# Splitting weights into high and low parts by casting and adding DMAs instead of on VectorE, in a two-block transformer kernel

## The chip, the core and the metric

The kernel runs on one core of a Trainium2 chip. A core has TensorE (PE in the profile, its weight loads PEld), VectorE (DVE), ScalarE (ACT), GpSimd (POOL) and SyncE (SP), each with its own in-order instruction queue; they wait for each other by semaphores only. 16 DMA engines move data between the memory off the core (DRAM in the code) and the two memories on it, SBUF and PSUM (128 partitions each; TensorE writes to PSUM). The metric is the device time of one execution in microseconds. It is given as the median of several executions; differences of about 0.2% can be told from no difference in this kernel.

## The reference

One sequence of 512 tokens with 1024 features passes two transformer blocks in float32. Cut to what matters:

```python
# block 1
h = rmsnorm(x, norm_mix)
x = x + hybrid_mixer(h, w_in, ...)            # gated spatial mixing + gated delta rule (4 heads), then @ w_out
m = rmsnorm(mem, norm_mem)                    # 256 memory tokens
x = x + memory_cross_attention(rmsnorm(x, norm_xa), m, xa_wq, xa_wk, xa_wv, xa_wo)
x = x + squared_relu_mlp(rmsnorm(x, norm_ffn), ffn_w1, ffn_w2)      # 1024 -> 4096 -> 1024
x = rmsnorm(x, norm_final)
# block 2
proj = rmsnorm(x, norm_mix_g_2) @ w_in_2      # split into the inputs of mLSTM and attention, and g_a, g_b
y_a, y_b = mlstm(...), sliding_window_attention(...)
x = x + (sigmoid(g_a) * (y_a @ w_branch_a_2) + sigmoid(g_b) * (y_b @ w_branch_b_2)) @ w_out_2
x = x + squared_relu_mlp(rmsnorm(x, norm_mlp_g_2), w_up_2, w_down_2)
x = x + sigmoid(rmsnorm(x, norm_ple_g_2) @ w_ple_gate_2) * (p_2 @ w_ple_proj_2)
out = rmsnorm(x, final_norm_g_2)
```

About 36 million float32 weights, some 146 MB, are read once each.

## The kernel before

The residual stays in SBUF as `x_fm`, 128 partitions x 8 feature tiles x 512 tokens. Every product with a weight goes through TensorE in the type `float32r`, which keeps fewer mantissa bits than float32. So both operands are held in two parts: a high part, rounded to `float32r`, and a low part, the remainder. `mm3` makes three products of them (L220 high x high, L221 and L222 the mixed ones) into one PSUM tile.

Weights are packed in DRAM in *granules* of 256 output columns x 1024 rows; `wgran` loads one in two halves of 512 KB (128 partitions x 4 k tiles x 256 columns, 4 KB per partition), each by one call of `wload`. A half goes through three tiles of the pool `wp`: the raw weight `wr` (2 buffers), the high part `wh` and the low part `wl` (3 buffers each). SP issues the load of `wr` (L200), ACT casts it to `wh` (L203), VectorE subtracts (`wl = wr - wh`, L204). There are 281 such casts and subtractions. In the first granule of all, `pieces` splits the first half into 1 and 3 k tiles, with the loads of `x` between them.

`proj_fm` multiplies a granule with the feature-major operand: two output tiles of 128 features x 512 tokens, each the sum of 8 k tiles x 3 products, so 48 products of 512 columns a granule; the second half of the granule is read last in each tile. There the weight is the stationary operand and the low part stands in L222. `proj_tm` makes token-major tiles (weight as moving operand, 256 columns; low part in L221). PSUM tiles of these projections are `psd`, three buffers. ACT and VectorE evacuate them; in the MLP (`ffn`) by a ReLU on VectorE (L804), a square on ACT (L805) and a split of the result into two parts (`split_sb`, L261 on ACT, L262 on VectorE).

POOL has little to do: sums of squares for the norms (`sq_acc`, L276), masks of the delta rule's heads (`dn_head`: `slg`, `dT`, `dA`, and the product with the gate `do`) and of the mLSTM's heads (`ml_head`: `E`, L1047), and a few others.

The order of instructions on each engine is set ahead of time by a scheduler of the framework, from dependencies, buffers and its own cost estimates. On an engine nothing passes an instruction that waits.

Of the kernel before, what the change touches and what calls it, by code (L numbers as in the profile page):

```python
# [9 lines left out]
F32 = mybir.dt.float32  # L10
F32R = mybir.dt.float32r
I32 = mybir.dt.int32
AF = mybir.ActivationFunctionType
ALU = mybir.AluOpType
AX = mybir.AxisListType
PSUM = bass.MemoryType.PSUM

P = 128
# [7 lines left out]
# columns of the packed per-feature vectors  # L26
# [8 lines left out]
# packed rows, replicated over the partitions by the load  # L35
# [8 lines left out]
# masks over [128, 128], and per-block masks over [128, 32] (one block of 32 columns per block of 32 rows)  # L44
# [20 lines left out]
class Kern:  # L65
    def __init__(self, tc, ctx, D, out, dbg=None):
# [3 lines left out]
        self.wp = ctx.enter_context(tc.tile_pool(name="wp", bufs=3))  # L70
# [27 lines left out]
    def psums(self):  # L98
        """four banks for the small products of a phase."""
        return self.tc.tile_pool(name=self.uid("pc"), bufs=2, space=PSUM)  # L100
# [4 lines left out]
    def pair(self, sl, dt=F32R):  # L105
        """[128, 8, 512] operand in two slots."""
# [51 lines left out]
    def rsqrt(self, pool, v, n, tag):  # L158
        """1/sqrt(v) of a small tile [128, n]."""
# [12 lines left out]
    def softplus(self, pool, z, n, tag):  # L172
        """max(z, 0) + log1p(exp(-|z|)) of a small tile, log1p(e) = 2 atanh(e / (2 + e))."""
# [19 lines left out]
    def wload(self, src, kt, n, pieces=None):  # L193
        """src: DRAM [128, kt, n]; kt*n <= 1056."""
        nc = self.nc
        raw = self.t(self.wp, [P, kt, n], "wr", bufs=2)
        hi = self.t(self.wp, [P, kt, n], "wh", F32R)
        lo = self.t(self.wp, [P, kt, n], "wl", F32R)
        for c, then in pieces or [(slice(0, kt), None)]:
            nc.sync.dma_start(raw[:, c], src[:, c])  # L200
            if then:
                then()
            nc.scalar.copy(hi[:, c], raw[:, c])  # L203
            nc.vector.tensor_tensor(out=lo[:, c], in0=raw[:, c], in1=hi[:, c].bitcast(F32), op=ALU.subtract)  # L204
        return hi, lo

    def wgran(self, name, g, n=256, nk=8, pieces=None):
        """granule g of a packed weight: (hi, lo) accessors over k."""
# [8 lines left out]
    def mm3(self, ps, ah, al, bh, bl, first, last):  # L217
        """ps (+)= a^T b with operands in two parts."""
# [15 lines left out]
    def proj_fm2(self, w, xh, xl, tiles, evac):  # L234
        """as proj_fm, k outermost."""
# [21 lines left out]
    def split_sb(self, hi, lo, src, scale=None):  # L257
        """hi/lo of src * scale (src in SBUF or PSUM, scale per partition)."""
# [19 lines left out]
    def tok_rs(self, acc, tag, ntt=NB, eps=EPS, mul=None):  # L278
        """acc: [128, tokens] partial sums over partitions -> rsqrt(mean + eps) per token, [128, ntt];
        mul: per-token factor [128, ntt] on the mean."""  # L280
# [8 lines left out]
    def tok_bc(self, rs, tag, ntt=NB, out=None):  # L289
        """[128 tok, ntt] -> [128, tokens] replicated over partitions."""  # L290
# [1086 lines left out]
```

## Time and profile before

| | before |
|---|---|
| three runs, median (lowest to highest) | 1759.84 us (1758.4 to 1761.03) |
| span of the profiled execution, first to last instruction | 1755.6 us |
| TensorE busy | 1718.3 us, 98% |
| VectorE busy | 1012.1 us, 58% |
| ACT busy | 720.4 us, 41% |
| POOL busy | 147.7 us, 8% |
| mean granted TensorE clock | 0.994 of full speed |
| DMA | 155.09 MB, 27.3% of 16 engines' span on SP's queue |

The profile is one execution, and its own time is the span; the runs of the median are other executions and include what lies before the first and after the last instruction. Busy times of TensorE are those of pipelined matmuls with modelled ends, so that 98% doesn't mean peak speed. In rows of groups, `out<-in` names the tiles, then come partitions x elements and the count, the summed busy time, the mean duration in ns, and the idle time of the engine just before these instructions with what ended it. In rows of waits, "A <- B: t, n, m" says that A waited for B, t us in all, n times, m at most. In rows of the timeline come the start, the duration, engine, line, operation and tiles, and in brackets the idle time before it.

### The profile page before, as it was taken

Reading aid. Unit: us, or ns where it says so; the run is one execution under the profiler, and the core shown is the slowest. Engines: PE = TensorE matmul, PEld = TensorE weight load, DVE = VectorE, ACT = ScalarE, POOL = GpSimd, SP = SyncE. Lnnn points to the kernel's source line nnn. Section 1 sums busy time; section 2 is a strip of 40 time slices with the busy share of each in tenths; the row PEclk is TensorE's granted clock in tenths of the full one; section 3 lists DMA queues with packets and bytes.
Section 4 is the critical chain, followed back from the end, with each engine's and each line's share of the span. In section 5 each row is a group of like instructions: output and inputs, shape, how many; then the busy total and the mean of one; then the engine's idle time right before and its main releaser. Section 6 shows DMA issues by size and latency. Waiting matters only on the chain.

```text
span 1755.6 us, 22644 instructions
## 1 busy us (share of the span) xinstructions
PE 1718.3 (98%) x8740; PEld 1427.2 (81%) x8740; DVE 1012.1 (58%) x2039; ACT 720.4 (41%) x1254; POOL 147.7 (8%) x126
## 2 busy tenths in 40 slices
PE   8999999999999999999999999999999999999997
PEld 6987788878888888888889877788888888888876
DVE  6898887655543434447755589735555434344446
ACT  5344544544342323234454468623234423232343
POOL 2211311201000000011000000000120000000102
PEclk9999999999999999999999999999999999999998
DMA  5222223312222332232222211233232222223231
GB/s 196 86 73 63 73 90 101 102 49 79 90 97 96 96 96 97 96 96 73 75 73 82 74 59 37 85 96 97 91 100 85 93 90 95 96 96 108 90 102 61
DMA packets 49436, 155.09 MB, mean 88 GB/s; under 512 B 9392, under 2 KB 11696, under 8 KB 49328
## 3 DMA queue, kind: packets, MB, share of 16 engines
q1 hardware_dynamic: 49328, 153.64, 27.3%
q8 instruction: 69, 1.13, 0.3%
q14 instruction: 39, 0.32, 0.1%
HBM read 151.26 MB, written 2.10 MB: 87 GB/s over the span
## 4 chain that ended last, share of the span: by engine, by line
PE 84%; DVE 10%; ACT 3%; issue 1%; POOL 0%; DMA 0%; SPq 0%; DVEq 0%; ACTq 0%; POOLq 0%
PE psd L221 25%; PE psd L222 25%; PE psd L220 25%; DVE wl L204 1%; ACT wh L203 1%; PE c L563 1%; ACT lg L1154 1%; PE m L1064 1%; PE c L512 1%; DVE S L368 1%; DVE e L319 1%; PE po L1170 0%; DVE qs L1122 0%; PE lg L1143 0%; DVE S L1176 0%
## 5 line engine op out<-in xcount | busy, mean ns | idle before, releaser
L220 PE MATMUL psd<-S,wh 128*128 128x512 f32 (+1 forms) x1968 | 770.4, 392 | 6.1 <-ACT wh L203 6.1
L222 PE MATMUL psd<-S,wl 128*128 128x512 f32 (+1 forms) x1968 | 774.0, 393 | 1.4 <-DVE wl L204 1.4
L221 PE MATMUL psd<-S,wh 128*128 128x512 f32 (+1 forms) x1904 | 747.9, 393 | 0.3 <-DVE S L265 0.3
L204 DVE TENSOR_TENSOR wl<-wr,wh 128x1024 fp32r<-128x1024 f32 (+3 forms) x281 | 349.1, 1242 | 219.7 <-ACT wh L203 218.0
L203 ACT CAST wh<-wr 128x1024 fp32r<-128x1024 f32 (+3 forms) x281 | 292.0, 1040 | 434.0 <-PE psd L221 408.1
L220 PEld LDWEIGHTS psd<-S,wh 128*128 128x128 f32 x1968 | 373.5, 190 | 86.7 <-ACT wh L203 7.0
L222 PEld LDWEIGHTS psd<-S,wl 128*128 128x128 f32 x1968 | 372.3, 189 | 80.9 <-DVE wl L204 3.2
L221 PEld LDWEIGHTS psd<-S,wh 128*128 128x128 f32 x1904 | 359.6, 189 | 78.8 <-DVE S L265 1.7
L276 POOL TENSOR_TENSOR acc<-acc,sq 128x512 f32<-128x512 f32 (+1 forms) x47 | 67.8, 1442 | 917.7 <-ACT sq L274 917.3
L401 DVE TENSOR_TENSOR x_fm<-psd,x_fm 128x512 f32<-128x512 f32 x88 | 60.7, 690 | 138.0 <-PE psd L222 137.9
L221 PE MATMUL psd<-wl,S 128*128 128x256 f32 (+2 forms) x480 | 137.7, 287 | 0.6 <-DVE wl L204 0.6
L222 PE MATMUL psd<-wh,S 128*128 128x256 f32 (+2 forms) x480 | 136.4, 284 | 0.0
L220 PE MATMUL psd<-wh,S 128*128 128x256 f32 (+2 forms) x480 | 136.3, 284 | 0.0
L804 DVE SCALAR_TENSOR_TENSOR e<-psd,bc 128x512 f32<-128x512 f32 x64 | 44.2, 691 | 112.2 <-PE psd L222 109.3
L805 ACT ACTIVATE e<-e 128x512 f32<-128x512 f32 x64 | 40.4, 632 | 135.1 <-DVE e L804 135.1
L221 PEld LDWEIGHTS psd<-wl,S 128*128 128x128 f32 x480 | 90.3, 188 | 1.6 <-DVE wl L204 1.0
L220 PEld LDWEIGHTS psd<-wh,S 128*128 128x128 f32 x480 | 90.5, 189 | 0.5
L222 PEld LDWEIGHTS psd<-wh,S 128*128 128x128 f32 x480 | 90.6, 189 | 0.3
L262 DVE TENSOR_TENSOR S<-e,S 128x512 fp32r<-128x512 f32 (+1 forms) x84 | 56.7, 675 | 49.2 <-ACT S L261 49.2
L261 ACT CAST S<-e 128x512 fp32r<-128x512 f32 (+1 forms) x84 | 50.5, 601 | 42.9 <-POOL e L929 27.1
L264 ACT ACTIVATE S<-x_fm,vec 128x512 fp32r<-128x512 f32 x40 | 28.8, 721 | 55.8 <-DVE x_fm L401 37.1
L319 DVE SCALAR_TENSOR_TENSOR e<-e,vec,e 128x511 f32<-128x511 f32 (+2 forms) x60 | 46.6, 779 | 2.6 <-ACT e L316 2.2
(411 smaller groups left out, 1456.7 us busy)
## 6 DMA issues: line engine op xcount, KB each, us to landing
wr<-in_ffn_w_dram SPq DMA_DIRECT2D x64, 512.0 KB
wr<-in_w_up_dram SPq DMA_DIRECT2D x32, 512.0 KB
wr<-in_w_down_dram SPq DMA_DIRECT2D x32, 512.0 KB
wr<-in_w_in_qk_dram SPq DMA_DIRECT2D x16, 512.0 KB
wr<-in_w_in_v_dram SPq DMA_DIRECT2D x12, 512.0 KB
wr<-in_xa_wk_dram SPq DMA_DIRECT2D x8, 512.0 KB
wr<-in_xa_wv_dram SPq DMA_DIRECT2D x8, 512.0 KB
wr<-in_xa_wq_dram SPq DMA_DIRECT2D x8, 512.0 KB
```

Source lines behind the costliest of these rows:

```text
L203: nc.scalar.copy(hi[:, c], raw[:, c])
L204: nc.vector.tensor_tensor(out=lo[:, c], in0=raw[:, c], in1=hi[:, c].bitcast(F32), op=ALU.subtract)
L220: mm(ps, ah, bh, start=first, stop=False)
L221: mm(ps, ah, bl, start=False, stop=False)
L222: mm(ps, al, bh, start=False, stop=last)
L261: nc.scalar.copy(hi, src)
L262: nc.vector.tensor_tensor(out=lo, in0=src, in1=hi.bitcast(F32), op=ALU.subtract)
L276: eng.tensor_tensor(out=acc, in0=acc, in1=sq, op=ALU.add)
L319: nc.vector.scalar_tensor_tensor(out=c[:, s:], in0=xr[:, :T - s], scalar=w(j), in1=c[:, s:], op0=ALU.mult, op1=ALU.add)
L401: self.nc.vector.tensor_tensor(out=self.x[:, o], in0=ps, in1=self.x[:, o], op=ALU.add)
L804: nc.vector.scalar_tensor_tensor(out=t, in0=ps, scalar=0.0, in1=bc, op0=ALU.max, op1=ALU.mult)
L805: nc.scalar.activation(t, t, AF.Square)
```

## The change

`wload` no longer has a raw tile in the pool, except where `pieces` is given (the first half granule, whose raw tile lies in the slot S8). In all other calls a DMA issued by POOL loads the weight straight into `wh`, with the cast to `float32r` on the way; ACT writes the negated high part into `wl`; and a second DMA issued by POOL reads the same raw weight from DRAM again and adds it onto `wl`. The pool `wp` has 4 buffers of each tile instead of 3. The rest of the difference is comments taken out, by which line numbers move.

```diff
-        self.wp = ctx.enter_context(tc.tile_pool(name="wp", bufs=3))
+        self.wp = ctx.enter_context(tc.tile_pool(name="wp", bufs=4))
...
     def wload(self, src, kt, n, pieces=None):
         nc = self.nc
-        raw = self.t(self.wp, [P, kt, n], "wr", bufs=2)
         hi = self.t(self.wp, [P, kt, n], "wh", F32R)
         lo = self.t(self.wp, [P, kt, n], "wl", F32R)
-        for c, then in pieces or [(slice(0, kt), None)]:
-            nc.sync.dma_start(raw[:, c], src[:, c])
-            if then:
-                then()
-            nc.scalar.copy(hi[:, c], raw[:, c])
-            nc.vector.tensor_tensor(out=lo[:, c], in0=raw[:, c], in1=hi[:, c].bitcast(F32), op=ALU.subtract)
+        if pieces:
+            raw = self.slot(8, [P, kt, n])
+            for c, then in pieces:
+                nc.sync.dma_start(raw[:, c], src[:, c])
+                if then:
+                    then()
+                nc.scalar.copy(hi[:, c], raw[:, c])
+                nc.vector.tensor_tensor(out=lo[:, c], in0=raw[:, c], in1=hi[:, c].bitcast(F32), op=ALU.subtract)
+            return hi, lo
+        nc.gpsimd.dma_start(hi, src)
+        nc.scalar.activation(lo, hi.bitcast(F32), AF.Copy, scale=-1.0)
+        nc.gpsimd.dma_start(lo, src, accum_op=ALU.add)
         return hi, lo
```

In the built program 279 of 281 half granules take the new way: 279 casts and 279 subtractions go, 279 scaled copies on ACT and 558 DMAs on POOL come, and SP loses 279 loads. The products on TensorE are the same in number; since the scheduler sees other durations, the order of some instructions on every engine moves.

How the loads stand in the first MLP. Before, on SP's queue (the tiles are the raw halves of two granules; in brackets the semaphores waited for: DMAHW are those of SP's loads, the others those of engines):

```order
L200 DMA wr_953_5454<-in_ffn_w1_dram 128x1024 [waits DMAHW7_49,DVE_49]
L200 DMA wr_960_5520<-in_ffn_w1_dram 128x1024 [waits DMAHW0_49,DVE_49]
L200 DMA wr_963_5526<-in_ffn_w1_dram 128x1024 [waits DMAHW1_49,DVE_49]
L200 DMA wr_970_5592<-in_ffn_w1_dram 128x1024 [waits DMAHW2_49,DVE_49]
L200 DMA wr_973_5598<-in_ffn_w1_dram 128x1024 [waits DMAHW3_49,DVE_49]
```

Now, on POOL's queue, two granules of the same weight (DMASW are the semaphores of POOL's DMAs):

```order
L208 DMA wh_861_5359<-in_ffn_w1_dram 128x1024 [waits DMASW2_49,PE_49]
L208 DMA wh_863_5364<-in_ffn_w1_dram 128x1024 [waits DMASW3_49,PE_49]
L210 DMA wl_862_5360<-in_ffn_w1_dram 128x1024 [waits DMASW4_49,Activation_49]
L210 DMA wl_864_5365<-in_ffn_w1_dram 128x1024 [waits DMASW5_49,Activation_49]
L208 DMA wh_869_5429<-in_ffn_w1_dram 128x1024 [waits DMASW6_49,PE_49]
L208 DMA wh_871_5434<-in_ffn_w1_dram 128x1024 [waits DMASW7_49,PE_49]
L210 DMA wl_870_5430<-in_ffn_w1_dram 128x1024 [waits DMASW0_49,Activation_49]
L210 DMA wl_872_5435<-in_ffn_w1_dram 128x1024 [waits DMASW1_49,Activation_49]
```

Each load has become two, the queue has moved from SP to POOL, and a granule stands as both high halves, then both low halves. A high half waits for TensorE's release of the buffer, a low half for ACT's copy.

How POOL's own work stands among them in the mLSTM. Before, on POOL (E is the decay matrix of a head, to be masked; S a memset beside it):

```order
L1047 TENSOR_TENSOR E0_1224_7293<-E0_1224_7293,masks_115 128x512 [waits PE_49,Activation_49,Pool_49]
L966 MEMSET S6_1318_7803 128x4x2 [waits DVE_49,PE_49,Activation_49]
L1047 TENSOR_TENSOR E1_1294_7734<-E1_1294_7734,masks_115 128x512 [waits Activation_49]
L966 MEMSET S7_1388_8236 128x4x2 [waits PE_49,DVE_49,Activation_49,Pool_49]
L1047 TENSOR_TENSOR E0_1364_8167<-E0_1364_8167,masks_115 128x512 [waits Activation_49]
```

Now, on POOL, the first such mask and what stands around it:

```order
L208 DMA wh_1145_7474<-in_w_in_v2_dram 128x1024 [waits DMASW2_49,PE_49]
L1053 TENSOR_TENSOR E0_1091_7160<-E0_1091_7160,masks_112 128x512 [waits Activation_49,Pool_49]
L208 DMA wh_1147_7479<-in_w_in_v2_dram 128x1024 [waits DMASW3_49,PE_49]
L210 DMA wl_1146_7475<-in_w_in_v2_dram 128x1024 [waits DMASW4_49,Activation_49]
L210 DMA wl_1148_7480<-in_w_in_v2_dram 128x1024 [waits DMASW5_49,Activation_49]
L208 DMA wh_1182_7667<-in_w_in_o_dram 128x1024 [waits DMASW6_49,PE_49]
L208 DMA wh_1184_7672<-in_w_in_o_dram 128x1024 [waits DMASW7_49,PE_49]
L210 DMA wl_1183_7668<-in_w_in_o_dram 128x1024 [waits DMASW0_49,Activation_49]
L972 MEMSET S6_1179_7664 128x4x2 [waits PE_49,DVE_49,Activation_49,Pool_49]
```

The mask of a head now stands behind a load that waits for TensorE, and weight loads stand behind the mask.

How POOL's queue begins. Now (acc and sq belong to the sum of squares of the first norm; in_w_in_u is the first weight, whose second half and second granule these are):

```order
L208 DMA wh_4_92<-in_w_in_u_dram 128x1024
L208 DMA wh_6_101<-in_w_in_u_dram 128x1024
L208 DMA wh_8_106<-in_w_in_u_dram 128x1024
L282 ISA
L282 TENSOR_TENSOR acc_14_121<-acc_14_121,sq_15_127 128x512 [waits Activation_49]
L210 DMA wl_5_93<-in_w_in_u_dram 128x1024 [waits Activation_49]
L210 DMA wl_7_102<-in_w_in_u_dram 128x1024 [waits Activation_49]
L210 DMA wl_9_107<-in_w_in_u_dram 128x1024 [waits Activation_49]
L282 TENSOR_TENSOR acc_14_121<-acc_14_121,sq_16_132 128x512 [waits Pool_49]
```

Before, POOL's queue held only the sums there and SP issued these loads between those of `x`. The low halves of the first weight now stand behind the first sum, and the second sum behind them.

## The prediction

> **What bounds the kernel now.** I read the page's busy shares first, then the chain, then the stretches, then what TensorE waits for, and last the rows of one weight granule.
>
> ```profile
> span 1755.6 us, 22644 instructions
> PE 1718.3 (98%) x8740; PEld 1427.2 (81%) x8740; DVE 1012.1 (58%) x2039; ACT 720.4 (41%) x1254; POOL 147.7 (8%) x126
> PE 84%; DVE 10%; ACT 3%; issue 1%; POOL 0%; DMA 0%; SPq 0%; DVEq 0%; ACTq 0%; POOLq 0%
> ```
>
> TensorE is busy for 1718.3 of 1755.6 us, so 37.3 us of idle time is all that any relief of another engine can give back, however large that relief is. POOL, at 8%, is nearly free; the change gives it work. The three runs have a median of 1759.84 us, 4.2 us above the span of the profiled execution; I make the sum against 1755.6 and add 4.2.
>
> The stretches (each row: us, then busy time of PE, PEld, DVE, ACT, POOL, then clock, DMA share and GB/s) show two kinds of stage:
>
> ```profile
> 176.00:264.00 88.00, 82.20 (x559) 72.81 (x558) 75.64 (x235) 42.21 (x115) 22.40 (x19) 0.96 0.28 83
> 264.00:352.00 88.00, 84.72 (x543) 74.54 (x542) 61.03 (x140) 43.92 (x85) 14.11 (x9) 1.00 0.32 99
> 616.00:704.00 88.00, 88.00 (x381) 71.15 (x380) 35.62 (x40) 25.80 (x32) 0.00 (x0) 1.00 0.30 96
> 1584.00:1672.00 88.00, 88.00 (x381) 71.40 (x380) 36.25 (x43) 26.66 (x34) 6.22 (x4) 1.00 0.30 96
> ```
>
> In the MLP (the last two rows) TensorE has no idle time at all and VectorE is at 40%; taking work from VectorE there can give nothing. In the mixer with the delta rule (first row) VectorE is at 86%, yet TensorE's idle time is 5.8 us. What TensorE waits for, by the view of waits:
>
> ```profile
> PE psd L220 <- ACT wh L203: 6.1, 2, 5.3
> PE c L512 <- DVE kdec L543: 3.4, 3, 1.6
> PE m L1064 <- DVE PT L1052: 2.6, 4, 0.8
> ...
> PE psd L222 <- DVE wl L204: 1.4, 3, 0.7
> ...
> PE psd L221 <- DVE wl L204: 0.6, 1, 0.6
> ...
> PE pss L1165 <- DVE lg L1159: 0.2, 1, 0.2
> ```
>
> The subtraction, `wl` of L204, costs TensorE 2.0 us in the whole kernel; the 6.1 us behind the cast are at the very start, 5.3 of them at once, where the change keeps the old way.
>
> **The change part by part.** What is removed and what takes its place on ACT and VectorE:
>
> ```profile
> L204 DVE TENSOR_TENSOR wl<-wr,wh 128x1024 fp32r<-128x1024 f32 (+3 forms) x281 | 349.1, 1242 | 219.7 <-ACT wh L203 218.0
> L203 ACT CAST wh<-wr 128x1024 fp32r<-128x1024 f32 (+3 forms) x281 | 292.0, 1040 | 434.0 <-PE psd L221 408.1
> L264 ACT ACTIVATE S<-x_fm,vec 128x512 fp32r<-128x512 f32 x40 | 28.8, 721 | 55.8 <-DVE x_fm L401 37.1
> L261 ACT CAST S<-e 128x512 fp32r<-128x512 f32 (+1 forms) x84 | 50.5, 601 | 42.9 <-POOL e L929 27.1
> L276 POOL TENSOR_TENSOR acc<-acc,sq 128x512 f32<-128x512 f32 (+1 forms) x47 | 67.8, 1442 | 917.7 <-ACT sq L274 917.3
> ```
>
> 1. VectorE loses 279 of 281 subtractions, 279 x 1.24 = 346 us. Nearly all lies beside TensorE. Gained: the 2.0 us of direct waits, and part of the waits for other VectorE work (15 rows of that view from `kdec` to `lg`, 18.0 us), which end earlier when no subtractions stand among them. Bounds 0 and 18; I take 5, since these chains are a VectorE instruction after another with a subtraction only now and then between. Together -7.
>
> 2. ACT trades 279 casts for 279 scaled copies. A scaled activation is 0.12 us longer than a cast at 512 columns (721 against 601), so 1.05 to 1.2 us each; at most 279 x 0.12 = 33 us more on an engine that is 41% busy. At no cost; what hides it is TensorE's work. Without that cover it would be 0.1 us a half granule. The copy also waits for the landing of `hi` instead of a free buffer, 4 to 5 us longer, and behind it on ACT stand the evacuations; TensorE has three PSUM buffers of 5.6 us each before it would wait for those, so this too I cost at nothing in the MLP.
>
> 3. The loads. Before, one load of 512 KB a half granule (4 of the 8 k tiles); now two, both issued by POOL, and the second reads its destination too. Between them stands ACT's copy. Nothing in this trace shows a DMA issued by POOL, a casting DMA or an adding one. The chain before is short, since the raw tile was loaded long before: ACT's cast waits only for TensorE to release the buffer.
>
> ```profile
> 636.74 1.05 ACT L203 CAST wh<-wr 128x1024 fp32r<-128x1024 f32 x1 [6.10 <-PE psd L221]
> 639.52 1.05 ACT L203 CAST wh<-wr 128x1024 fp32r<-128x1024 f32 x1 [1.73 <-PE psd L221]
> 647.89 1.05 ACT L203 CAST wh<-wr 128x1024 fp32r<-128x1024 f32 x1 [7.31 <-PE psd L221]
> ```
>
> First and third row are the same half of successive granules: a granule lasts 11.15 us, 48 products of 0.232. The second half is released 2.78 us after the first, at the granule's end. With four buffers a half of granule n+1 lands where that half of granule n-1 was. Counted from the end of n-1, the low part of the second half is first needed by product 15 of granule n+1, after 11.15 + 14 x 0.232 = 14.4 us. In those 14.4 us now lie, one after another: issue and landing of `hi`, ACT's copy, issue and landing of `lo`. Call their sum L. From that product 34 remain, 7.9 us, to the end of n+1, two granules after the start; so where L is over 14.4 a granule lasts (L + 7.9)/2.
>
> The landing of a plain load is seen at one place, where ACT really waited for it:
>
> ```profile
> 302.89 0.33 SPq L200 DMA_DIRECT2D wr<-in_w_out_b_dram  x1
> ...
> 304.56 0.33 SPq L200 DMA_DIRECT2D wr<-in_w_out_b_dram  x1
> ...
> 306.80 1.05 ACT L203 CAST wh<-wr 128x1024 fp32r<-128x1024 f32 x1 [1.81 <-DMA wr<-in_w_out_b_dram]
> ...
> 309.47 1.05 ACT L203 CAST wh<-wr 128x1024 fp32r<-128x1024 f32 x1 [0.65 <-DMA wr<-in_w_out_b_dram]
> q1 hardware_dynamic: 49328, 153.64, 27.3%
> ```
>
> 3.9 us from issue to use for the one, 4.9 for the next, issued while the first was in flight. The queue's row (packets, MB, share of 16 engines) gives the transfer itself: 0.273 x 1755.6 us for 153.64 MB, 1.64 us for 512 KB. Lower bound of L: both loads as SP's are, 3.9 + 1.05 + 3.9 = 8.9. Upper: POOL needs as long to write out a DMA as for one of its own 128x512 operations (1.4 us, L276) on top, both land as the slower one, `lo` takes four times the transfer, and each waits for another such: 1.4 + 4.9 + 1.2 + 1.4 + 4.9 + 3 x 1.64 + 1.64 = 20.4. I take: 0.7 us for each issue (between SP's 0.33 and 1.4); `hi` 4.4; the copy 1.1 with 0.2 for its semaphore; `lo` 4.4 + 1.64 for the second read = 6.0; and 2.1 for transfers of the other half in the way, since the DMA share goes from 0.30 to 0.60 by the count of loads and to 0.90 with the second read. L = 5.1 + 1.3 + 6.7 + 2.1 = 15.2, nearer to the middle than to an end because no row speaks for either. A granule then lasts 11.55 us, 0.40 more. Stretches at 90 GB/s and over are eleven of 88 us, 87 granules: +35 us. At the bounds: 0, and (20.4 + 7.9)/2 = 14.15, +3.0 x 87 = +261.
>
> The Trainium skill (Collectives: The Full Stack, "The bandwidth ceiling: the fold count and why AG ≠ RS ≠ AR") says that an add in the DMA engines is no slower as such but reads two sources on one ring and so moves half as much. No run here shows it yet. By it `lo` is an estimated 1.64 us longer than a copy, as I took it; taken as free, L would be 13.6 and this term nothing.
>
> 4. POOL's queue. Before, SP issued the loads and waited for VectorE with nothing behind it that was urgent, and POOL had only its own work. Now 558 issues stand in POOL's order among that work, each with a wait: `hi` for TensorE's release, `lo` for ACT's copy. Behind them stand the masks and squares.
>
> ```profile
> SPq L200 <- DVE wl L204: 1320.9, 252, 24.6
> POOL E L1047 <- ACT E L1046: 74.2, 3, 40.7
> DVE PT L1052 <- POOL E L1047: 2.2, 3, 0.7
> ```
>
> Before, POOL stood ready for ACT's exponential every time but one (74.2 us idle), and VectorE then waited for POOL, TensorE for VectorE (`PT` above). Now the mask of a head comes behind a `hi` that waits up to a granule's part. Some 28 such POOL operations feed a head's chain (delta rule 24, mLSTM 4); bounds 0 (all find their waits over) and 28 x 4.9 (each finds a landing ahead of it) = 137. I take a wait of 1.5 us at one in three, since the order interleaves rather than stacks them: +14.
>
> 5. The start. The first half granule goes as before; its second half now needs `hi`, copy and `lo`, and `lo` stands on POOL behind the first square:
>
> ```profile
> 8.34 1.31 POOL L276 TENSOR_TENSOR acc<-acc,sq 128x512 f32<-128x512 f32 x1 [6.88 <-ACT sq L274]
> 11.88 1.03 ACT L203 CAST wh<-wr 128x1024 fp32r<-128x1024 f32 x1
> 12.95 2.10 DVE L204 TENSOR_TENSOR wl<-wr,wh 128x1024 fp32r<-128x1024 f32 x1
> 14.86 0.39 PE L220 MATMUL psd<-S,wh 128*128 128x512 f32 x1
> ```
>
> The low part was ready at 15.05 us and used about then. If ACT's copy stands where its cast did, to 12.9, `lo` lands 3.9 to 6.7 later, at 17 to 20: a stall of 2 to 5, less what VectorE's lighter list gives back after it. I take +3.
>
> Sum: -7 + 0 + 35 + 14 + 3 = +45, a span of 1800.6, and 1805 us with the 4.2.
>
> **The rivals.** *All hidden.* L stays under 14.4 and POOL's waits are over when their work comes: -7 + 3 = -4, about 1756 us, and down to 1743 if all the VectorE waits go too. For it: the lower bound of L, 8.9, is not much farther from 15.2 than the upper one; the point is 14.4. Against: two unseen DMA kinds, and four loads a granule where two were. The Trainium skill (DMA: Bandwidth & Descriptors, "Anatomy of one DMA") fits 2.0 us + bytes/436e3 for a DMA that GpSimd issues, an estimated 3.2 us here; the plain load of the trace took 3.9 by another path, so it is not tested; by it L would be 7.7 and this rival would win.
>
> *The DMA engines become the bound.* Two plain passes and two adding ones fill a granule when `hi` + `lo` exceed 5.6 us of transfer in place of 4.9; a little is enough. At three passes for `lo`, 2 x (1.64 + 4.92) = 13.1 us a granule, +2.0 x 87 = +174, about 1944 us with the other terms. At two for `hi` and four for `lo` 19.7 us a granule, 140 granules, 2760 us. For it: the MLP's share of 0.30 leaves room for three passes and no more. Against: no row shows a cast or an add to be slower per byte.
>
> *About even*: gains and POOL's waits cancel, within 0.2% (3.5 us, about what a measurement of this kernel can tell).
>
> **How the numbers follow.** Slower by the latency of the loads, 1763 to 1880: 0.40, the likeliest, so 1805. Bound by DMA engines, above 1880: 0.31, a third of it above 2250. All hidden and faster: 0.16. Even: 0.13. Faster 0.16, same 0.13, slower 0.71. The range from 1743 to 2250 leaves out 0.02 below and 0.10 above; the likeliest case alone is 1763 to 1880.
>
> **What would show it.** Right: TensorE waits of around 1 us a granule for `wl` whose releaser is a DMA in the MLP's stretches; VectorE's busy time near 666 us; SP nearly empty; a DMA share of 0.6 to 0.9 in the MLP; POOL idle behind TensorE and ACT. Step 3 is wrong if the MLP's granules still last 11.15 us; step 4 if POOL's masks start no later behind ACT's exponentials. The forecast fails most easily on the price of an adding DMA, which nothing before shows, and which acts on every granule.

## The result, and the profile after

The changed kernel takes 1866.38 us (median of four runs, 1862.23 to 1876.61), the kernel before in the same session 1759.12 (1756.89 to 1761.03): a ratio of 1.0609, 95% interval 1.0579 to 1.064. It is 107 us slower; the forecast was 1805 us, 46 slower. The direction was right, the size was not: 107 us of change against the 45 of the forecast's sum.

The profiled execution of the changed kernel: its page (span, busy times, the queue that carries the weights with packets, MB and share of 16 engines), the mean clock of both kernels, and four stretches beside one of before that was not yet shown (PE, PEld, DVE, ACT, POOL busy, then clock, DMA share, GB/s).

```profile
span 1860.5 us, 22723 instructions
...
PE 1764.6 (95%) x8740; PEld 1462.4 (79%) x8740; DVE 690.4 (37%) x1760; ACT 715.9 (38%) x1254; POOL 530.5 (29%) x684
...
q0 software_dynamic: 80352, 290.62, 69.5%
```

Mean clock, the kernel before:

```profile
core 0: 1755.6 us, clock 0.994
```

and after:

```profile
core 0: 1860.5 us, clock 0.969
```

Stretches after:

```profile
176.00:264.00 88.00, 78.34 (x460) 65.79 (x460) 66.30 (x209) 39.87 (x112) 31.87 (x37) 0.93 0.46 104
264.00:352.00 88.00, 74.93 (x464) 71.06 (x463) 35.67 (x130) 29.63 (x67) 20.27 (x26) 0.75 0.61 130
352.00:440.00 88.00, 76.84 (x387) 64.66 (x387) 28.44 (x64) 34.51 (x58) 25.73 (x31) 0.93 0.74 162
616.00:704.00 88.00, 88.00 (x381) 71.15 (x380) 16.39 (x24) 25.58 (x31) 22.83 (x32) 1.00 0.83 189
```

The third of them before:

```profile
352.00:440.00 88.00, 87.84 (x424) 70.03 (x423) 46.72 (x75) 38.34 (x69) 6.35 (x5) 1.00 0.20 66
```

Two things are to be read here. VectorE lost 322 us of work (1012.1 to 690.4), as the change intends, and TensorE's products are the same 8740. But TensorE's idle time grew from 37.3 to 95.9 us, +58.6, and its busy time from 1718.3 to 1764.6, +46.3, for the same products; the two make the span's +104.9. The fall of the clock accounts for the busy part: (1 - 0.969) x 1860.5 - (1 - 0.994) x 1755.6 = 47 us. And the MLP, on which the forecast laid 35 us, lost nothing in this stretch: 88.00 of 88 us busy, 381 products as before, at a DMA share of 0.83. The largest part of what went wrong lies between 176 and 440 us: from 264 to 352 us there are 74.93 us busy at a clock of 0.75 where the kernel before had 84.72 at 1.00.

What TensorE waits for after, by the view of waits (us in total, times, longest):

```profile
PE pss L290 <- DVE acc L282: 12.4, 5, 3.9
PE psd L227 <- DMA wl<-in_xa_wv_dram: 12.4, 3, 6.3
PE psd L226 <- ACT wh L205: 9.7, 2, 7.9
PE c L518 <- DVE kdec L549: 5.3, 2, 4.0
PE psd L227 <- DMA wl<-in_w_in_gate_dram: 4.6, 1, 4.6
```

The first row is the end of a norm (the last sum of squares), the second the memory's values, the third the start. To see where the time falls, the delay against the kernel before at the same instructions of both traces, in us (the last kernels are from the experiments below):

| place (us in the kernel before) | after | POOL free | memory as before | both | both, norms on VectorE |
|---|---|---|---|---|---|
| gated spatial mix, last (95.8) | 15.9 | 5.0 | 14.7 | 7.4 | 8.9 |
| delta rule's last head (307.1) | 27.0 | 7.8 | 24.2 | 7.3 | 8.6 |
| cross attention's first exponential (347.6) | 69.8 | 33.8 | 33.3 | 13.8 | 9.1 |
| first ReLU of the first MLP (457.2) | 79.9 | 40.9 | 43.7 | 22.3 | 12.2 |
| last product with w_out_2 (1323.0) | 96.1 | 56.5 | 64.7 | 37.3 | 22.9 |
| last ReLU of the second MLP (1592.5) | 99.4 | 59.2 | 70.2 | 39.9 | 24.0 |

In the changed kernel 42.8 of the 105 us appear between the last head and the cross attention. Not all of that is lost there. By the timelines 158 of the 192 products of the memory's values still stand behind the last head in the changed kernel, and 8 in the kernel before; 150 products of 0.119 us are some 18 us of work that has only moved behind this place. So the row of the last head understates the delay where the values come late. From the spatial mix to the cross attention both kernels do nearly the same work (the heads, the memory's keys and values, the mixer's output), and over that whole stretch the delay grows by 53.9 us, half of all that is lost.

### The profile page after: what moved, and what is told of

The parts are those of the page before. It is cut to its first block, busy times and chain, and to the rows that moved or that the text cites. A ratio compares the mean times of both kernels' runs of the same rounds, so it can differ in the third digit from the quotient of the medians.

```text
span 1860.5 us, 22723 instructions
## 1 busy us (share of the span) xinstructions
PE 1764.6 (95%) x8740; PEld 1462.4 (79%) x8740; DVE 690.4 (37%) x1760; ACT 715.9 (38%) x1254; POOL 530.5 (29%) x684
## 3 DMA queue, kind: packets, MB, share of 16 engines
q0 software_dynamic: 80352, 290.62, 69.5%
## 5 line engine op out<-in xcount | busy, mean ns | idle before, releaser
L226 PE MATMUL psd<-S,wh 128*128 128x512 f32 (+1 forms) x1968 | 782.2, 398 | 10.9 <-ACT wh L205 9.7
L227 PE MATMUL psd<-S,wh 128*128 128x512 f32 (+1 forms) x1904 | 752.9, 396 | 0.2 <-DVE S L268 0.2
L209 ACT ACTIVATE wl<-wh 128x1024 fp32r<-128x1024 f32 (+2 forms) x279 | 293.6, 1053 | 723.4 <-DMA wh<-in_ffn_w_dram 212.0
L226 PEld LDWEIGHTS psd<-S,wh 128*128 128x128 f32 x1968 | 378.1, 192 | 91.7 <-ACT wh L205 10.5
L227 PEld LDWEIGHTS psd<-S,wh 128*128 128x128 f32 x1904 | 365.7, 192 | 77.4 <-DVE S L268 0.7
L227 PE MATMUL psd<-wl,S 128*128 128x256 f32 (+2 forms) x480 | 140.0, 292 | 16.9 <-DMA wl<-in_xa_wv_dram 12.4
L226 PE MATMUL psd<-wh,S 128*128 128x256 f32 (+2 forms) x480 | 139.3, 291 | 2.7 <-DMA wh<-in_xa_wv_dram 2.7
L228 PE MATMUL psd<-wh,S 128*128 128x256 f32 (+2 forms) x480 | 139.8, 292 | 0.0
L210 POOL DMA_DIRECT2D wl<-in_ffn_w_dram x64 | 56.0, 875 | 145.7 <-ACT wl L209 141.8
L226 PEld LDWEIGHTS psd<-wh,S 128*128 128x128 f32 x480 | 93.7, 196 | 3.4 <-issue 2.9
L228 PEld LDWEIGHTS psd<-wh,S 128*128 128x128 f32 x480 | 94.2, 196 | 0.2
L208 POOL DMA_DIRECT2D wh<-in_ffn_w_dram x64 | 36.4, 569 | 118.8 <-PE psd L228 115.3
L282 POOL TENSOR_TENSOR acc<-acc,sq 128x512 f32<-128x512 f32 (+1 forms) x47 | 60.9, 1295 | 29.4 <-ACT sq L280 27.8
L271 DVE SCALAR_TENSOR_TENSOR S<-x_fm,vec,S 128x512 fp32r<-128x512 f32 x40 | 36.1, 907 | 77.5 <-ACT S L270 77.5
```

What stands on the lines that cost most here:

```text
L208: nc.gpsimd.dma_start(hi, src)
L209: nc.scalar.activation(lo, hi.bitcast(F32), AF.Copy, scale=-1.0)
L210: nc.gpsimd.dma_start(lo, src, accum_op=ALU.add)
L226: mm(ps, ah, bh, start=first, stop=False)
L227: mm(ps, ah, bl, start=False, stop=False)
L228: mm(ps, al, bh, start=False, stop=last)
```

## The experiments

Each was run beside the kernel before on the same chip. Theory A blames POOL's in-order queue, B the memory's stage, C the price of the two DMAs in every granule (step 3 of the forecast), D ACT's queue.

| kernel | ratio to before | 95% interval |
|---|---|---|
| changed kernel | 1.0609 | 1.0579 to 1.064 |
| e1, POOL only for loads | 1.0352 | 1.0327 to 1.0377 |
| e2, start as before | 1.0559 | 1.0525 to 1.0594 |
| e3, memory's stage as before | 1.0384 | 1.0343 to 1.0425 |
| e4, only the MLPs changed, three buffers | 1.1411 | 1.1358 to 1.1465 |
| e8, e1 and e3 together | 1.0241 | 1.0201 to 1.0281 |
| e6, no add | 1.0325 | 1.0286 to 1.0364 |
| e7, kernel before, loads issued by POOL | 1.0057 | 1.0034 to 1.008 |
| e9, kernel before, two stalls put in | 1.0087 | 1.0061 to 1.0112 |
| e10, e8 with the copy on POOL | 1.2008 | 1.1969 to 1.2048 |
| e11, e8 with the norms on VectorE | 1.0151 | 1.0124 to 1.0178 |
| e12, e11 with the start as before | 1.0123 | 1.0092 to 1.0154 |
| e13, a fifth buffer in the memory's stage | 1.0597 | 1.0551 to 1.0644 |

**e1: POOL only for loads.**

```
-nc.gpsimd.tensor_tensor(...)     # masks, gate, spatial mixing
+nc.vector.tensor_tensor(...)
-eng = nc.gpsimd if k < KT - 1 else nc.vector
+eng = nc.vector                  # sums of squares
```

> The changed kernel, with every tensor operation of POOL (masks, the squares' sums, gates) given to VectorE, so that POOL's queue holds only the weight DMAs. Theory A: POOL's in-order queue is a main cost, because masks and sums stand behind loads that wait, and loads behind masks that wait. Then the waits of TensorE for the last square (12.4 us in the trace after) and for the delta rule's chain (about 20 us) mostly go, with part of the clock lost after them: 1825 to 1845 us. Theory B: the loss is in the memory's keys and values, where a granule of 256 tokens lasts half as long and four half-granule buffers do not cover the loop of loads: 1855 to 1868. Theory C: each granule pays the price of the two DMAs (my step 3): 1860 to 1870, no change, or slightly slower since VectorE has 100 operations more.

1824.64 us, 0.0257 of the time before better than the changed kernel, some 45 us, at the lower end of A's range. How the queue costs is seen in the changed kernel's own rows on POOL in the delta rule:

```profile
138.78 0.59 POOL L208 DMA_DIRECT2D wh<-in_w_in_v_dram  x1 [4.08 <-PE psd L227]
139.39 1.30 POOL L573 TENSOR_TENSOR dT<-dM,masks 128x512 f32<-128x512 f32 x1
```

A load waits 4.08 us for TensorE to release a buffer, and the mask `dT` of a head's chain stands behind it. The delay up to the last head fell from 27.0 to 7.8 us, and 10.9 of these 19.2 us are there at the spatial mix already (15.9 to 5.0): the queue is also what delays the start. The other wait that A had named, for the last sum of squares, mostly stayed, though POOL no longer makes the sums. Of 12.4 us there are left

```profile
PE pss L290 <- DVE acc L282: 9.6, 4, 3.6
```

The edit does two things at once: it empties POOL's queue, and it gives the operations to an engine that is faster at them (the mask `dT` takes 1.36 us on POOL and 0.68 on VectorE, by the means of both traces). The 24 operations of the delta rule's heads would be some 16 us shorter by that, if all of them lay on the path; this run does not separate the two.

**e2: the start as before.** The raw tiles lie in slots that are free then.

```
+if name == "w_in_u":
+    raw = ...;  nc.sync.dma_start(raw, src);  nc.scalar.copy(hi, raw)
+    nc.vector.tensor_tensor(out=lo, in0=raw, in1=hi..., op=ALU.subtract);  return hi, lo
```

> The changed kernel, with the four half granules of w_in_u (the first products) loaded, cast and subtracted as before. The trace after stands 12.8 us behind the trace before when the first 84 us are over. If this is the start alone (the casting DMAs compete with x, and the low parts come late): 1851 to 1855 us. If the delay is regained or caused later by POOL's queue (theory A): 1860 to 1866.

1863.58 us, with an interval that overlaps the changed kernel's: not told apart from no change. In its trace the delay at the spatial mix is 6.1 us instead of 15.9, and at the first exponential 66.4 instead of 69.8: most of the start's gain is lost again before the cross attention.

**e3: the memory's stage as before.** The same edit for `xa_wk`, `xa_wv` and `w_out_b`.

> The changed kernel, with xa_wk, xa_wv (the memory's keys and values) and w_out_b loaded, cast and subtracted as before; everything else stays split by DMAs. Between 307 and 457 us of the kernel before the changed one lost 53 us. Theory B: nearly all of it comes back, with the halved clock of that stage: 1810 to 1830 us. Theory A: only what those loads blocked in POOL's queue, 5 to 15 us: 1850 to 1861. Theory C: 10 granules of some 140 stop paying, 107 x 10/140 = 8 us: 1858.

1829.98 us, some 40 us better than the changed kernel, at the upper end of B's range. The stretch shown above at 74.93 us and a clock of 0.75, in this kernel:

```profile
264.00:352.00 88.00, 83.81 (x581) 78.67 (x581) 54.56 (x154) 39.14 (x82) 7.99 (x7) 0.88 0.30 91
```

581 products in the place of 464. C, which spreads the loss evenly, allowed 8 us.

**e4: only the two MLPs changed.** Everything else as before; the raw tiles take the room of the fourth buffers.

```
+if name not in ("ffn_w1", "ffn_w2", "w_up_2", "w_down_2"):
+    (load raw, cast, subtract, as before)
-tile_pool(name="wp", bufs=4)
+tile_pool(name="wp", bufs=3)
```

> The kernel before, with only the weights of the two MLPs split by DMAs (64 granules of 140), three buffers of each part. Theory C, my step 3: each of these granules pays, 0.4 us or more: 1785 us or above. Theories A and B: the MLP hides the loads (its granules lasted 11.15 us in the trace after as in the one before) and only the squares at its ends come later: 1757 to 1766. With three buffers instead of four the loop of loads, 10.8 us by the trace after, has some 8.8 to 11 us of cover, so up to 20 us more would speak for the buffers and not against A and B.

2016.51 us: far outside every expectation, for with three buffers I had seen at most 20 us more. The rows of one loop in its MLP, on POOL's timeline:

```profile
647.37 0.55 POOL L215 DMA_DIRECT2D wh<-in_ffn_w_dram  x1 [6.62 <-PE psd L234]
...
652.45 0.88 POOL L217 DMA_DIRECT2D wl<-in_ffn_w_dram  x1 [1.59 <-ACT wl L216]
```

On TensorE's timeline, a wait for the low part in each granule:

```profile
642.62 0.51 PE L235 MATMUL psd<-S,wl 128*128 128x512 f32 x1 [2.71 <-DMA wl<-in_ffn_w_dram]
...
658.10 0.80 PE L235 MATMUL psd<-S,wl 128*128 128x512 f32 x1 [2.51 <-DMA wl<-in_ffn_w_dram]
...
673.26 0.50 PE L235 MATMUL psd<-S,wl 128*128 128x512 f32 x1 [2.45 <-DMA wl<-in_ffn_w_dram]
```

The page's row on the landing of its adding DMAs (issues, KB each, median us):

```profile
wl<-in_ffn_w_dram POOLq DMA_DIRECT2D x64, 512.0 KB, 5.5
```

From the issue of `hi` at 647.37 to the landing of `lo` at 652.45 + 5.5 = 657.95 are 10.6 us, and the product that needed it started at 658.10. With three half-granule buffers the first half of granule n is released by product 36 of its 48, and the buffer takes the second half of granule n+1, whose low part is used about product 14: 26 products of 0.232, 6.0 us of cover. A granule should last 11.15 + 10.6 - 6.0 = 15.75 us; by the three rows of TensorE it lasts 15.3. The forecast's model of the loop holds, then, and my expectation had the cover of three buffers wrong. In the changed kernel, with four buffers, the cover is 14.4 us. Its rows of one chain, the two issues on POOL's timeline:

```profile
649.90 0.55 POOL L208 DMA_DIRECT2D wh<-in_ffn_w_dram  x1 [2.38 <-PE psd L228]
...
655.10 0.88 POOL L210 DMA_DIRECT2D wl<-in_ffn_w_dram  x1 [1.85 <-ACT wl L209]
```

The copy between them, on ACT's timeline:

```profile
653.74 1.06 ACT L209 ACTIVATE wl<-wh 128x1024 fp32r<-128x1024 f32 x1 [7.38 <-DMA wh<-in_ffn_w_dram]
```

And the landing of `lo`, by the page:

```profile
wl<-in_ffn_w_dram POOLq DMA_DIRECT2D x64, 512.0 KB, 5.6
```

655.10 + 5.6 - 649.90 = 10.8 us, 3.6 under the cover: that is why its MLP stands at 88.00 of 88. (Here `hi` took 3.8 us from issue to use; the page's median of its landing is 4.6, and with that the sum is 11.6, still under the cover.) The fourth buffer, which the change brought along, is what hides the loads there.

**e8: e1 and e3 together.**

> Both at once: POOL holds only weight DMAs (its tensor operations on VectorE), and xa_wk, xa_wv and w_out_b go as before. If the two causes are separate, the gains add: 1866 - 42 - 36 = 1788 us. If what POOL's queue cost lay mostly in the memory's stage, they overlap: 1800 to 1825. What is then still left above the kernel before (some 29 us by the sum) would be the start (about 9 us by the places of the first products) and stalls at the delta rule's heads and the norms, with the clock after them.

1799.82 us: between the two expectations, at the low end of the second. The single gains, 0.0257 and 0.0225, would add to 0.0482; together they are 0.0368. About a quarter of what they cure is common to both; probably POOL's queue also held back the loads of the memory's stage, which no run shows by itself. Above the kernel before 0.0241 are left, 42 us. TensorE's largest wait in this kernel:

```profile
PE pss L300 <- DVE acc L292: 11.3, 4, 3.6
```

The wait at the norms is still there, though POOL has no part in it now.

**e6: no add.** It leaves out the addition (the low part is the weight itself).

```
-nc.gpsimd.dma_start(lo, src, accum_op=ALU.add)
+nc.gpsimd.dma_start(lo, src)
```

> The changed kernel with the second DMA only casting, not adding (it leaves out the addition: the low part then is the weight itself, so the output is another one). It prices the add by itself. In the trace after an adding DMA keeps POOL for 0.875 us and lands in 5.6 us, a casting one 0.569 and 4.6. If the add's second read loads the DMA engines and the loop (theories B and C): the DMA share falls from 0.70 to about 0.5 or less, the waits for xa_wv shrink, 1835 to 1855 us. If the order of POOL's queue is what counts (theory A): 1858 to 1868. If the MLP is hidden anyway, its granules stay at 11.15 us.

1816.75 us, some 50 us less than the changed kernel, more than I had expected. The page of this kernel, with two casts a half granule: the queue (packets, MB, share of 16 engines) and the landings (issues, KB each, median us):

```profile
q0 software_dynamic: 80352, 290.62, 54.0%
...
wh<-in_ffn_w_dram POOLq DMA_DIRECT2D x64, 512.0 KB, 3.7
wl<-in_ffn_w_dram POOLq DMA_DIRECT2D x64, 512.0 KB, 3.8
```

The same rows of e7 (below), where POOL issues plain loads:

```profile
q0 software_dynamic: 39920, 145.31, 25.6%
...
wr<-in_ffn_w_dram POOLq DMA_DIRECT2D x64, 512.0 KB, 3.7
```

The rows price the DMAs by themselves. A plain 512 KB load keeps the 16 engines for 0.256 x 1773.9 x 0.524/145.31 = 1.64 us, a casting one 0.540 x 1810.4 x 0.524/290.62 = 1.76, and both land in 3.7 us: the cast costs almost nothing. The pair with an add takes 2 x 0.695 x 1860.5 x 0.524/290.62 = 4.66, so the add takes 2.90, 1.8 times a plain load. (The Trainium skill, Collectives: The Full Stack, "The bandwidth ceiling: the fold count and why AG ≠ RS ≠ AR", has an add read two sources and so move half as much; 1.8 is near it.) The low part lands 1.8 us later than a plain load, and the 0.875 us of POOL per issue fall too; this run does not separate these.

**e7: the kernel before, its loads issued by POOL.**

```
-nc.sync.dma_start(raw[:, c], src[:, c])
+(nc.sync if pieces else nc.gpsimd).dma_start(raw[:, c], src[:, c])
```

> The kernel before, with its raw loads issued by POOL instead of SP (281 issues, no cast and no add by DMA, ACT's cast and VectorE's subtraction as before). Theory A: POOL's in-order queue alone costs, since each load waits there for a raw buffer with masks and sums behind it: 1775 to 1800 us. Rival: the queue costs only together with the longer loop of two DMAs, which makes its waits long; two raw tiles ahead, POOL's waits are over when its other work comes: 1757 to 1766.

1772.32 us, some 10 us slower: between the two ranges. In its trace, which is of a run of 1775.66 us, 11.7 us of delay are there at the spatial mix and 19.2 from the cross attention to the end. The queue costs something by itself, mostly at the start, where loads wait for VectorE ahead of the first squares; in the changed kernel its cure was worth four times that, with the longer loop's waits in it and the faster operations of e1.

**e9: the kernel before with two stalls put in.** A chain of 7 subtractions on POOL starts at an evacuation of the memory's keys, one of 9 at an evacuation of the first MLP; after the granule one 128x1 product waits for the chain's end.

```
+st = self.stall(slot, t, n, ops)      # POOL: st = t - t; then ops times st = st - st
+nc.tensor.matmul(ps[:, 0:1], st[:, 0:P], self.ones[:, 0:1], start=True, stop=True)
```

> The kernel before, with two single waits put into TensorE's order: a chain of subtractions on POOL starts at an evacuation, and one 128x1 product waits for its end. One wait, some 6 to 9 us, lies in the memory's keys (products of 256 columns between the heads), the other, some 8 us, in the first MLP (512 columns). It asks where the halved clock of the changed kernel comes from. Theory: from the stalls themselves, and it lasts where products are short: about 16 us of stalls, 2 to 4 us of halved clock in the MLP, and 10 to 15 us lost in the memory's stage, where the clock stays at 0.50 for 15 us or more: 1785 to 1795 us. Rival: the halved clock came with the traffic of the DMAs, not with a stall: the stalls cost their length and a few us, 1772 to 1780, and no long stretch at 0.50 follows either.

1776.75 us, in the rival's range of time, but because the first stall came out shorter than planned. In the memory's stage TensorE waited 1.82 us only, for a mask behind the chain, 5 us after a wait of 1.64 that the kernel before has at this place too (1.63 us). In the MLP it waited 7.38:

```profile
243.26 1.16 PE L527 MATMUL c<-dq,dk 128*128 128x128 f32 x8 [1.64 <-DVE kdec L558]
...
248.43 1.89 PE L578 MATMUL c<-masks,dT 128*128 128x16 f32 x8 [1.82 <-POOL dT L582]
...
535.42 0.58 PE L170 MATMUL pss<-ones,S 128*128 128x1 f32 x2 [7.38 <-POOL S L165]
```

The stretch behind the wait of 1.82 us:

```profile
250.00:262.00 12.00, 12.00 (x57) 12.00 (x57) 4.18 (x8) 2.21 (x5) 2.75 (x3) 0.50 0.32 90
```

The same stretch of the kernel before:

```profile
250.00:262.00 12.00, 12.00 (x107) 11.37 (x106) 9.50 (x27) 6.19 (x14) 0.00 (x0) 1.00 0.36 109
```

Behind these two waits TensorE runs 12 us at half clock, busy without a gap, with 57 products in the place of 107; with the first of them alone the kernel before keeps its full clock. The delay at the last head is 9.9 us. There is no more DMA traffic here than before, 0.32 against 0.36, so the halved clock does not need it. That part of the rival falls. The MLP's stall cost 10.5 us by the trace, 3 more than its 7.4.

**e10: e8 with the copy on POOL.**

```
-nc.scalar.activation(lo, hi.bitcast(F32), AF.Copy, scale=-1.0)
+nc.gpsimd.tensor_scalar(out=lo, in0=hi.bitcast(F32), scalar1=-1.0, scalar2=None, op0=ALU.mult)
```

> The kernel with both cures (1800 us), with the negated copy of the high part made by POOL instead of ACT. Theory D: what is left comes largely from ACT's queue, where the copy waits for a landing (up to 6 us) with the norms' scalings and squares and the evacuations behind it; TensorE then waits 3.6 to 3.9 us at each norm, and the clock halves for up to 10 us. With the copy on POOL the waits for the last sum (11.3 us) and the halved clock after them mostly go: 1775 to 1790 us, although the loop of loads gets longer by some 1.6 us (a POOL operation of 512 columns takes 1.3 us, so 2.6 for 1024). Rival: the rest is the traffic and the start; nothing is gained: 1796 to 1806, or more if the longer loop no longer fits in the 14.4 us.

2112.98 us, far slower. Of the rival only its last clause, that the longer loop might not fit, came true, at a price that neither theory gave; on D this run says nothing. POOL's timeline in its MLP:

```profile
704.62 1.10 POOL L218 DMA_DIRECT2D wh<-in_ffn_w_dram  x2 [0.42 <-issue]
710.46 2.77 POOL L219 TENSOR_SCALAR wl<-wh 128x1024 fp32r<-128x1024 f32 x1 [4.75 <-DMA wh<-in_ffn_w_dram]
713.53 0.91 POOL L220 DMA_DIRECT2D wl<-in_ffn_w_dram  x1 [0.30 <-POOL wl L219]
714.16 3.11 POOL L219 TENSOR_SCALAR wl<-wh 128x1024 fp32r<-128x1024 f32 x1
717.57 0.90 POOL L220 DMA_DIRECT2D wl<-in_ffn_w_dram  x1 [0.30 <-POOL wl L219]
```

TensorE's longer wait in two successive granules there:

```profile
705.05 0.50 PE L238 MATMUL psd<-S,wl 128*128 128x512 f32 x1 [1.76 <-DMA wl<-in_ffn_w_dram]
...
719.16 0.50 PE L238 MATMUL psd<-S,wl 128*128 128x512 f32 x1 [1.82 <-DMA wl<-in_ffn_w_dram]
```

POOL issues two casts, sits through their landing, and makes both copies and both issues one after another: a granule lasts 14.1 us instead of 11.15. Neither the loop of one half alone nor POOL's share (53%) shows this; the queue's order does.

**e11: e8 with the norms on VectorE.** Scaling to the high part, and the squares, go from ACT to VectorE; the copy stays on ACT.

```
-nc.scalar.activation(hi, src, AF.Copy, scale=scale);  nc.scalar.activation(sq, src, AF.Square)
+nc.vector.tensor_scalar(out=hi, in0=src, scalar1=scale, ...);  nc.vector.tensor_tensor(out=sq, in0=src, in1=src, op=ALU.mult)
```

> The kernel with both cures (1800 us), with the norms' scalings and squares on VectorE, and the negated copy still on ACT. Theory D: the norm's boundaries no longer stand behind a copy that waits for a landing, and TensorE's 11.3 us there fall below 4, with less halved clock: 1780 to 1792 us; other evacuations still stand behind the copies. Rival (traffic and start): 1796 to 1806.

1788.52 us, 0.009 less than e8, some 16 us, inside D's range. The wait at the norms, 11.3 us in e8, is now 0.8. In the kernel before, where ACT made the scalings and squares as well, it was 1.8, so that their length alone does not explain it. Now, and then before:

```profile
PE pss L309 <- DVE acc L301: 0.8, 1, 0.8
```

```profile
PE pss L284 <- DVE acc L276: 1.8, 2, 0.9
```

The mean clock is 0.993 instead of 0.986. How ACT's queue costs is seen in the changed kernel at the end of the first MLP. ACT's timeline:

```profile
892.25 1.08 ACT L209 ACTIVATE wl<-wh 128x1056 fp32r<-128x1056 f32 x1 [5.98 <-DMA wh<-in_w_in_o_dram]
893.24 0.71 ACT L270 ACTIVATE S<-x_fm,g 128x512 fp32r<-128x512 f32 x1
```

VectorE's:

```profile
894.64 0.69 DVE L282 TENSOR_TENSOR acc<-acc,sq 128x512 f32<-128x512 f32 x1
```

TensorE's:

```profile
895.48 1.83 PE L290 MATMUL pss<-ones,acc 128*128 128x1 f32 x8 [3.85 <-DVE acc L282]
```

And a stretch of 3 us behind it:

```profile
899.00:902.00 3.00, 3.00 (x11) 2.63 (x11) 1.38 (x10) 0.00 (x0) 0.00 (x0) 0.50 0.80 155
```

ACT waits 5.98 us for the landing of the next phase's weight; the last scaling and square of the norm stand behind; TensorE waits 3.85 us, and then runs at half clock.

**e12: e11 with the start as before.**

> The last kernel (POOL only for loads, the norms on VectorE, xa_wk, xa_wv and w_out_b as before; 1788.5 us), with w_in_u as before too. Alone, the start as before moved the changed kernel by 3 us only, since the memory's stage behind it was slow for reasons of its own. If the start's 9 us are real and only hidden there, they come through now: 1776 to 1782 us. If they are made up elsewhere in any case: 1785 to 1790.

1782.05 us: at the upper end of the range in which the start's gain comes through, but the intervals of e11 and e12 overlap, so this is not shown. In this trace the clock fell to 0.986 again, which hides about what the start brought.

**e13: a fifth buffer in the memory's stage.**

```
+if name in ("xa_wk", "xa_wv") and self.nmem % 5 == 2:
+    both = self.slot(7, [P, 2, kt, n], F32R);  hi, lo = both[:, 0], both[:, 1]
```

> The changed kernel with a fifth pair of half-granule tiles while the memory's keys and values (xa_wk, xa_wv) are loaded: every fifth half granule there uses a tile that is free in this stage. It asks whether that stage is bound by the loop of loads or by the DMA engines. The loop is 10.7 us (0.55 + 3.3 + 1.1 + 0.3 + 5.5, from the trace after); four half granules of 256 columns cover 48 + 14 products of 0.119 = 7.4 us of it, five some 10.2. Loop theory: most of the stage's loss goes, with its halved clock: 1835 to 1852 us. Theory of the DMA engines: cast and add keep the 16 engines for about 4.7 us a half granule, TensorE needs 2.85, and a fifth tile brings at most a few us: 1858 to 1868.

1863.82 us, no change. The waits for the values' low part, 12.4 us in the changed kernel, are down to one in this stage:

```profile
357.57 0.38 PE L232 MATMUL psd<-wl,S 128*128 128x256 f32 x1 [3.06 <-DMA wl<-in_xa_wv_dram]
```

The stretches around it run at a DMA share of 0.9:

```profile
340.00:360.00 20.00, 14.55 (x114) 13.97 (x113) 4.64 (x15) 6.66 (x9) 5.69 (x8) 0.96 0.90 190
360.00:380.00 20.00, 17.68 (x93) 15.36 (x93) 4.83 (x8) 7.93 (x12) 6.32 (x9) 0.87 0.93 216
```

The delay at the cross attention is 68.9 us, against 69.8. So the loop of loads, as I had worked it out, is not what bounds this stage. A half granule needs 4.66 us of the engines and, with 256 memory tokens, 24 products of 0.119, 2.85 us, of TensorE: that speaks for the DMA engines, and the share of 0.9 agrees, but while the keys are multiplied, from 260 to 300 us, the share is 0.39 to 0.46 and the clock 0.57 to 0.66, so the engines are not the bound all through.

## Why the prediction was wrong in size, step by step

*Step 1, VectorE relieved, -7.* The relief is there (690.4 us busy, 666 forecast), the gain is not: the direct waits for the subtraction are gone, and the waits for `kdec` went from 3.4 to 5.3 us. That the engine with the removed work was off the path was read rightly.

*Step 2, ACT's copy, 0: the cover failed.* The step named the hazard (the copy waits for a landing, evacuations stand behind it) and covered it by TensorE's three PSUM buffers "in the MLP". It did not ask what happens where a phase ends and TensorE needs ACT's next output at once. Taking the norms off ACT (e11) was worth some 16 us.

*Step 3, the loads, +35: the step failed in two ways.* L came out as 10.8 us, not 15.2: in the chain shown `hi` lands 3.8 us after its issue where 0.7 + 4.4 were taken (the landing counts from the issue), `lo` 5.6 where 0.7 + 6.0 were, and the 2.1 us for other transfers in the way were nothing, at a DMA share of 0.83 (by the page's median of 4.6 for `hi`, L is 11.6 and the other transfers some 0.9, against the 3.7 of e6). L was under 14.4, the point that the forecast gave, and the 87 granules of 11.15 us lost nothing that can be seen (TensorE waits once for a low part of the first MLP, 0.6 us). But the sum counted only granules of 512 columns. The memory's keys and values use the same 512 KB in half the time. From the spatial mix to the cross attention the changed kernel lost 53.9 us, e3 only 18.6, and some 40 us came back in e3 altogether. In the rival of the DMA engines the limit was worked out for 5.6 us a half granule; with the 2.85 of this stage the forecast's own 1.64 + 3.28 us would have been over it.

*Step 4, POOL's queue, +14: mis-sized.* Some 45 us came back in e1, of which some 20 are common with the memory's stage. The step counted masks behind waits. It left out the loads behind masks, the start, where e1 took 10.9 us off, and what follows a wait in the clock. The gain of e1 has in it that the operations are faster on VectorE, so 45 us is the most that this run puts down to the queue.

*Step 5, the start, +3: mis-sized.* The delay at the spatial mix was 15.9 us, 6.1 with the start as before and 5.0 with POOL free; in the whole kernel e2 was not told apart from the changed one.

*No step: the clock.* 47 of the 105 us are TensorE's clock, and the sum had no term for it, although its stretches were quoted with a column for the clock. The waits behind steps 2, 4 and 5 cost more than their length for this reason: after a stall the next products run at half clock. e9 shows that stalls do it in a kernel with the old traffic.

*The sign.* 35 of the forecast's 45 us were the loads of the 512-column granules, which cost nothing. That the kernel came out slower, and within the forecast's likeliest case, is in good part luck: other stages and the clock filled the place of this term.

Of the rivals, *all hidden* is true of the MLP and false elsewhere; loads that POOL issues land in 3.7 us where nothing is added (e7, e6), near the 3.9 of its lower bound. *The DMA engines become the bound* is false of the MLP and may be part of the truth for the memory's values.

What stays open: some 22 us between e12 and the kernel before. In the trace of e12, 27.1 us longer than that of the kernel before, 12.6 us are idle time of TensorE and 14.5 busy time at the lower clock. What brings them about, the doubled loads of the other weights or the traffic of the add, no run separates. Open too is how the loads of the memory's weights cost their 40 us: e13 speaks against the loop, and the share of 0.9 for the DMA engines in a part of the stage only. None of the variants beats the kernel before, which leaves TensorE idle for 37.3 us in all.

## What to carry to other kernels

Work that was moved here from an engine off the path onto queues gained nothing and added waits; so ask of each queue that it joins what stands behind the waiting instruction, first of all where one phase ends and the next begins. Work out a loop of loads for the stage that uses its bytes fastest, not for the one that is seen most, and count the buffers: here four hid a loop of 10.8 us completely and three made a granule last 15.3 us instead of 11.15. Price a stall of TensorE above its length, by what the clock does behind it.

## What was not expected of the hardware

*The clock stays low behind stalls in the stage of short products.* A wait of the changed kernel, in a head's chain:

```profile
253.44 2.07 PE L518 MATMUL c<-dq,dk 128*128 128x128 f32 x8 [3.96 <-DVE kdec L549]
```

A stretch behind it:

```profile
260.00:270.00 10.00, 10.00 (x48) 10.00 (x49) 2.63 (x10) 1.43 (x3) 2.14 (x2) 0.50 0.36 58
```

The same of the kernel before, where other products stand in it, at full clock:

```profile
260.00:270.00 10.00, 10.00 (x85) 9.82 (x85) 8.99 (x35) 6.28 (x18) 1.20 (x1) 1.00 0.32 105
```

TensorE is busy throughout and stays at half clock, weight loads included (PEld 10.00 of 10). The Trainium skill (TensorE: Matmul & The Clock Gate, "Part 1: The HAM clock gate (the "warmup" mystery)") has the clock fall after an idle window of about 3.4 us and come back after one busy window of the same length. Here it fell behind waits of 1.64 and 1.82 us, 5 us apart (e9), and stayed down for at least 12 us of busy time; behind the 3.96 us above it stayed down until some 282 us, by stretches of 2 us. The measurement decides. In the MLP the clock was back within some 7 us (e9). Which property of the products keeps it down was not tried.

*A casting load is nearly free, an adding one is not.* 1.76 and 2.90 us of the engines for 512 KB, against 1.64 for a plain one; 3.7 and 5.5 us to landing, against 3.7; 0.569 and 0.875 us of POOL for the issue.
